# One hybrid streaming layer on one core: retention with one transposition and products in half-height pieces of the array, the keys' lower parts stored once, and the weight sums' results in PSUM banks of their own

## The chip, the core and the metric

The kernel runs on one core of a Trainium2 chip. The time is device time in microseconds (us), the median of several runs. Engines are named as in the profile: PE (TensorE: matmuls and transpositions), PEld (its weight loads), DVE (VectorE), ACT (ScalarE), POOL (GpSimd), SP (the queue that issues the DMAs).

## The reference

One layer over 1024 prompt frames and 32 sample frames, model width 1024, eight heads. What the change touches is the score product of the differential attention and the retention:

```python
qa = rmsnorm(qa.reshape(B, T, A_HEADS, 2, A_DIM), g_qn)      # A_DIM 64, two maps per head
ka = rmsnorm(ka.reshape(B, T, A_HEADS, 2, A_DIM), g_kn)
s = jnp.einsum('bqhcd,bkhcd->bhcqk', q_blk, ka) * scale      # chunk-causal mask, softmax, p0 - lam * p1
...
def retention_chunk(q, k, v, s0, d_mat, q_decay):            # R_DK 64, R_DV 128
    inner = jnp.einsum('...ihd,...jhd->...hij', q, k) * d_mat
    o = jnp.einsum('...hij,...jhe->...ihe', inner, v)
    return o + jnp.einsum('...ihd,...hde->...ihe', q, s0) * q_decay[:, :, None]
s_next = chunk_decay * s + einsum('jhd,jhe->hde', k * k_decay, v)
```

Around it stand a projection to 8192 columns ahead (one block of weights for attention and one for retention per head), and behind it the output projection, a SwiGLU of width 2816 and a gated embedding. Outputs are the layer's result, the keys and values, and the retention states.

## The kernel before

**Stages.** Up to about 1083 us runs one planned stage (`stream`): 72 attention units (head h, tile i; tiles 0 to 7 are 128 prompt frames each, tile 8 is the 32 sample frames) and 72 retention units four units behind. Behind it come the output projection and the SwiGLU's first half (`stream_bc`, to about 1660 us), then the rest.

**What sets the order.** Both stages are written as Python generators. A planner (`Flow`) runs at build time: each step yields an estimated cost on an engine (`V`, `S`, `G`, `M` for DVE, ACT, POOL, PE), or `get`/`put` of a buffer, and the order in which the planner starts the steps becomes the order of each engine's instructions. On the chip every engine runs its list in that order.

**Numbers in two parts.** Operands of the large products are split into an upper fp16 part and a lower one. A projected tile takes three fp16 matmuls per 128 rows of depth (L713 to L715).

**Attention unit** (`unit_a`, `attend`). The queries `q4[:, m]` of map m hold the upper part in one half of the partitions and the lower part in the other (map 0: upper in 0 to 63; map 1: upper in 64 to 127). The key tile `kT` has four planes: the upper part of each map, written into both halves, and the lower part of each map, again in both halves. Six fp16 transpositions (L1045) turn queries and keys. The scores of map m are one matmul over the upper plane (L850), on the diagonal a small matmul that adds the mask (L852), and one over the lower plane (L853), all 128 rows deep; keys are taken 512 at a time. Up to 512 keys (tiles 0 to 3) both maps go into the two banks of one `sc` tile, map 0 first; above that (tiles 4 to 8) each map has its own turn.

**Retention unit** (`retention`). All in fp32; a fp32 matmul shows as two records in the profile. `qk` holds queries and keys of a tile side by side (columns 0 to 127) and zeros behind them (128 to 191). Two transpositions (L1116, columns 0 to 127 and 64 to 191) and one copy of 256 columns (L1119) give `qT`: plane 0 one of them over the other, plane 1 the upper one's partner over zeros. The zeros make every product 128 rows deep: scores (L1126), queries times state (L1128, the state's lower 64 partitions are zeros too), and the state's increment (L1129, 128 columns of weights, of whose result half is used). L1134 adds scores times values.

**Scales in the second stage.** The sum of squares over the 128 partitions of a block of weights is one matmul of one column (`weight_scale`, L300). In `stream_bc` it writes column 511 of `ssb`, one PSUM bank for the whole stage, which also holds the RMSNorm's sums (L1543) and the scale row that L1558 writes and L1562 reads eight times.

Of the kernel before, what the change touches and what calls it, by code (L numbers as in the profile page):

```python
# [21 lines left out]
P = 128  # L22
# [48 lines left out]
def M(us):  # L71
    return {"M": us}
# [111 lines left out]
def kernel(  # L184
# [104 lines left out]
    def weight_scale(amax, n, gi, tag, pool=True, norm=False, total=False, at_bank=None):  # L289


        p2 = sm(n, tag + "p2", 3)
        if total:
            if at_bank is None:
                yield ("wait", "id")
            key, psum = at_bank or ("o", ps_o)
            yield ("get", key)
            yield M(0.06)
            ps = psum[:, 511:512] if at_bank else psum.tile([P, 512], F32, tag=key, name="mt")[:, 0:1]
            nc.tensor.matmul(out=ps, lhsT=ones16, rhs=amax, start=True, stop=True)  # L300
# [24 lines left out]
        return s, d  # L325
# [159 lines left out]
    with ExitStack() as pa:  # L485
# [38 lines left out]
        nc.gpsimd.memset(S2[64:128], 0.0)  # L524
        s02 = hp.tile([P, 2, P], F32, name="s02")
        nc.gpsimd.memset(s02[64:128], 0.0)

# [224 lines left out]
        def prep_head_a(h, w, e):  # L752
# [7 lines left out]
            s0 = s02[:, h % 2]  # L760
            nc.sync.dma_start(out=s0[0:64], in_=st0[h])
            gr = hp.tile([P, P], F32, tag="grn", name="grn", bufs=2)
# [9 lines left out]
        def cache_steps(h, dA, e):  # L772
# [46 lines left out]
            if h:  # L819
                yield ("wait", ("av", h - 1, NT - 1))  # L820
            kcs = hp.tile([P, 4, PAST], F16, tag="kcs", name="kcs")
# [17 lines left out]
        def attend(key, i, R, q4, sblocks, masked, vblocks, NK, sc_ap, do_ap):  # L839
# [3 lines left out]
            for ms in ((0, 1),) if NK <= 512 else ((0,), (1,)):  # L843
                yield ("get", "sc")
                yield M(len(ms) * (2 * NK / 2400.0 + 0.03))
                ps = ps_s.tile([P, 1024], F32, tag="sc", name="sc")
                for m in ms:
                    for b0, n, kts in sblocks:
                        o = ps[0:R, 512 * ms.index(m) + b0:512 * ms.index(m) + b0 + n]
                        nc.tensor.matmul(out=o, lhsT=q4[:, m, 0:R], rhs=kts[:, m], start=True, stop=False)  # L850
                        if masked and b0 + n == NK:
                            nc.tensor.matmul(out=o[:, n - 64:n], lhsT=mrow[:, 0:R], rhs=mneg, start=False, stop=False)  # L852
                        nc.tensor.matmul(out=o, lhsT=q4[:, m, 0:R], rhs=kts[:, 2 + m], start=False, stop=True)  # L853
                if m:
# [129 lines left out]
        def unit_a(h, i, ps, dA, e):  # L984
# [39 lines left out]
            if i == NT - 1:  # L1024
# [4 lines left out]
            yield S(384, 0.1)  # L1029
            st = wk.tile([P, 6, 2, 64], F16, tag="qst", name="qst")  # L1030
# [6 lines left out]
            nc.vector.tensor_tensor(out=st[0:R, 4:6], in0=zqk[:, 1].unsqueeze(2).broadcast_to([R, 2, 2, 64]),  # L1037
                                    in1=st[0:R, 2:4], op=ALU.subtract)
            yield ("put", "z")
            yield ("get", "o")  # L1040
            yield M(0.336)
            pt = ps_o.tile([P, 1024], F16, tag="o", name="t")
            ptv = pt[:, 0:768].rearrange("p (g c) -> p g c", g=6)
            for g in range(6):
                nc.tensor.transpose(out=ptv[:, g, 0:R], in_=st[0:R, g].rearrange("p a c -> p (a c)"), identity=id16[0:R, 0:R])  # L1045
# [63 lines left out]
        def retention(h, i, R, vr, e, box):  # L1109
            yield ("wait", ("rot", h, i))  # L1110
            yield ("get", "o")
            yield M(0.22)
            pr = ps_o.tile([P, 512], F32, tag="o", name="pr")

            for a in range(2):
                nc.tensor.transpose(out=pr[:, a * P:a * P + R], in_=qk[0:R, (h * NT + i) % NQ, 64 * a:64 * a + P], identity=id32[0:R, 0:R])  # L1116
# [7 lines left out]
            yield M(0.66)  # L1124
            por = ps_o.tile([P, 512], F32, tag="o", name="por")[0:R, 0:P]
            nc.tensor.matmul(out=pr[0:R, 256:256 + R], lhsT=qT[:, 0, 0:R], rhs=qT[:, 1, 0:R], start=True, stop=True)  # L1126
            if S_in is not None:
                nc.tensor.matmul(out=por, lhsT=qT[:, 1, 0:R], rhs=S_in, start=True, stop=False)  # L1128
            nc.tensor.matmul(out=pr[:, 384:512], lhsT=qk[0:R, (h * NT + i) % NQ, 0:P], rhs=vr[0:R], start=True, stop=True)  # L1129
            yield V(128)  # L1130
# [8 lines left out]
            Sn = S2[:, (h * NT + i) % 2]  # L1139
            Sq = Sn[0:64]  # L1140
            if S_in is None:
                nc.vector.tensor_scalar(out=Sq, in0=pr[0:64, 384:512], scalar1=gT, scalar2=None, op0=ALU.mult)
            else:
                nc.vector.tensor_tensor(out=Sq, in0=S_in[0:64], in1=pr[0:64, 384:512], op=ALU.add)
                yield V(128, 0.5)
                nc.vector.tensor_scalar(out=Sq, in0=Sq, scalar1=gT, scalar2=None, op0=ALU.mult)
# [286 lines left out]
    with ExitStack() as pc:  # L1433
# [18 lines left out]
        with ExitStack() as pw:  # L1452
# [8 lines left out]
            xfs, gus, dns, banks, done = [], {}, {}, {}, []  # L1461
            ssb = pss.tile([P, 512], F32, tag="ss", name="ss")

# [47 lines left out]
            def residual(c):  # L1511
# [28 lines left out]
                B = CW // 4  # L1540
                ps = ssb
                for b in range(4):
# [41 lines left out]
            def load_gu(j):  # L1584
# [47 lines left out]
            def load_dn(m):  # L1632
# [24 lines left out]
                nc.vector.tensor_tensor(out=am, in0=ams[:, 0:1], in1=ams[:, 1:2], op=ALU.add)  # L1657
                s, d = yield from weight_scale(am, 1, None, "dn", norm=True, total=True, at_bank=("sw", ssb))
                for st, js in sts:
# [159 lines left out]

            flow = Flow(dict(ps=7, ss=1, sw=1, w=3, st=2, pr=2, th=2, acc=2, sq=2))  # L1820
            del flow.buffers["w"][1:], flow.buffers["st"][1:]
# [209 lines left out]
```

## Time and profile before

| | |
|---|---|
| median of 3 runs | 1945.02 us (1944.85 to 1945.72) |
| profiled execution: time, and span from the first to the last instruction | 1944.48 us, 1942.7 us |
| busy: PE, DVE, ACT, POOL | 97%, 78%, 55%, 35% |
| matmul records | 14267 |
| DMA: traffic over the span | 147.43 MB, 76 GB/s |

The busy time of PE counts a matmul from its start to its modelled end, and these overlap: a matmul of 512 fp16 columns shows 0.38 us, but the next one starts 0.22 us behind it. So what a matmul costs on PE is read here from the distance between starts in the timeline, not from its duration. Forms are written K*M KxN: K rows and M columns of weights, K rows by N columns of moving data.

### The profile page before, as it was taken

How to read it: one execution, taken by the hardware profiler on the slowest of the kernel's cores; microseconds unless marked ns; L12 is line 12 of the kernel's file. 1: busy time of each engine (PE TensorE's matmuls, PEld its weight loads, DVE VectorE, ACT ScalarE, POOL GpSimd, SP SyncE). 2: the span in 40 equal slices, each digit the busy share in tenths (PEclk: the TensorE clock that was granted, in tenths of full speed). 3: DMA queues.
4: the chain of work that ended last, by engine and by line, in shares of the span. 5: the costliest groups of instructions: out<-in, count | busy, mean ns of one | idle time of the engine just before them, and what ended most of it. 6: DMA issues, size and time to landing. Idle time of an engine off the chain costs nothing.

```text
span 1942.7 us, 38400 instructions
## 1 busy us (share of the span) xinstructions
PE 1886.0 (97%) x14267; PEld 1219.2 (63%) x14267; DVE 1511.3 (78%) x3947; ACT 1065.4 (55%) x2788; POOL 688.8 (35%) x1169
## 2 busy tenths in 40 slices
PE   6899999999999999999999998999999999999999
PEld 3465555655555555556566685777777776666665
DVE  7888878787787777877887579999999986753364
ACT  6766666666666666665666345555555552111132
POOL 2654435454444454444542058322323210000010
PEclk9999999999999999999999998999999999999999
DMA  6222112111121121221113721222111107211031
GB/s 205 70 64 75 62 28 63 57 49 63 33 79 57 31 82 36 55 80 29 61 57 132 267 68 34 78 89 86 69 66 45 66 31 266 73 61 64 24 131 49
DMA packets 71947, 147.43 MB, mean 76 GB/s; under 512 B 25264, under 2 KB 52016, under 8 KB 63824
## 3 DMA queue, kind: packets, MB, share of 16 engines
q1 hardware_dynamic: 71760, 144.98, 22.4%
q8 instruction: 112, 1.84, 0.4%
q14 instruction: 75, 0.61, 0.1%
HBM read 113.61 MB, written 31.34 MB: 75 GB/s over the span
## 4 chain that ended last, share of the span: by engine, by line
PE 77%; DVE 11%; POOL 5%; ACT 4%; issue 2%; DMA 1%; SPq 0%; POOLq 0%; DVEq 0%; ACTq 0%
PE ps L471 9%; PE ps L472 9%; PE ps L473 9%; PE pj L713 8%; PE pj L715 8%; PE pj L714 8%; PE ps L1448 4%; PE ps L1447 4%; PE ps L1446 4%; ACT p L868 2%; PE sc L850 1%; PE t L897 1%; PE sc L853 1%; POOL qkr L749 1%; DVE nm L860 1%
## 5 line engine op out<-in xcount | busy, mean ns | idle before, releaser
L713 PE MATMUL pj<-w,xh 128*128 128x512 f16 x1024 | 390.1, 381 | 0.0
L714 PE MATMUL pj<-w,xh 128*128 128x512 f16 x1024 | 389.5, 380 | 0.0
L715 PE MATMUL pj<-w,xh 128*128 128x512 f16 x1024 | 389.3, 380 | 0.0
L471 PE MATMUL ps<-mixs,w 128*128 128x352 f16 (+1 forms) x960 | 261.9, 278 | 1.2 <-ACT pws L1324 1.2
L472 PE MATMUL ps<-mixs,w 128*128 128x352 f16 (+1 forms) x960 | 261.9, 278 | 0.0
L473 PE MATMUL ps<-mixs,w 128*128 128x352 f16 (+1 forms) x960 | 261.8, 278 | 0.0
L471 PEld LDWEIGHTS <-w 128*128 128x128 f16 x1728 | 170.2, 98 | 63.9 <-ACT mixs L1478 6.4
L473 PEld LDWEIGHTS <-w 128*128 128x128 f16 x1728 | 170.0, 98 | 54.2 <-issue 2.7
L472 PEld LDWEIGHTS <-w 128*128 128x128 f16 x1728 | 169.9, 98 | 51.7 <-issue 2.2
L715 PEld LDWEIGHTS <-xh 128*128 128x128 f16 x1024 | 100.4, 98 | 121.9 <-issue 1.7
L1581 POOL TENSOR_TENSOR st<-st 128x512 f32<-128x512 f32 x66 | 85.8, 1301 | 251.1 <-DVE w L1576 187.0
L868 ACT ACTIVATE p<-sc,nb,scs 128x256 f32<-128x256 f32 (+7 forms) x128 | 106.1, 829 | 83.3 <-POOL nb L862 61.1
L713 PEld LDWEIGHTS <-xh 128*128 128x128 f16 x1024 | 101.2, 99 | 76.3 <-issue 2.8
L472 PE MATMUL ps<-tT,w 128*128 128x352 f16 (+1 forms) x528 | 143.7, 277 | 2.6 <-DVE tT L1472 2.6
L714 PEld LDWEIGHTS <-xh 128*128 128x128 f16 x1024 | 100.4, 98 | 71.7 <-issue 1.1
L471 PE MATMUL ps<-tT,w 128*128 128x352 f16 (+1 forms) x528 | 143.8, 277 | 0.0
L473 PE MATMUL ps<-tT,w 128*128 128x352 f16 (+1 forms) x528 | 143.6, 277 | 0.0
L1576 DVE SCALAR_TENSOR_TENSOR w<-st,gus,w 128x512 f16<-128x512 f32 x132 | 140.5, 1065 | 0.1
L860 DVE TENSOR_REDUCE nm<-sc 128x2 f32<-128x256 f32 (+6 forms) x112 | 102.7, 917 | 24.1 <-PE sc L853 22.0
L1448 PE MATMUL ps<-a,w 128*128 128x352 f16 x312 | 97.5, 313 | 0.5 <-DVE w L1667 0.5
L1446 PE MATMUL ps<-a,w 128*128 128x352 f16 x312 | 97.5, 312 | 0.0
L1447 PE MATMUL ps<-a,w 128*128 128x352 f16 x312 | 97.5, 312 | 0.0
(430 smaller groups left out, 4856.1 us busy)
## 6 DMA issues: line engine op xcount, KB each, us to landing
st<-in_win_dram SPq DMA_DIRECT2D x30, 1024.0 KB, 5.0
st<-in_wgu_dram SPq DMA_DIRECT2D x22, 1024.0 KB, 4.9
st<-in_wdn_dram SPq DMA_DIRECT2D x16, 704.0 KB, 4.6
out_dram<-kv SPq DMA_DIRECT2D x64, 128.0 KB, 1.7
a_d<-a SPq DMA_DIRECT2D x9, 528.0 KB, 2.7
b<-a_d SPq DMA_DIRECT2D x9, 528.0 KB, 8.9
mixs<-mix_d SPq DMA_DIRECT2D x8, 528.0 KB, 5.8
pw_d<-pws SPq DMA_DIRECT2D x12, 352.0 KB, 5.0
```

Of the source, the lines that this page charges most:

```text
L471: nc.tensor.matmul(out=ps, lhsT=wh, rhs=ah, start=first, stop=False)
L472: nc.tensor.matmul(out=ps, lhsT=wh, rhs=al, start=False, stop=False)
L473: nc.tensor.matmul(out=ps, lhsT=wl, rhs=ah, start=False, stop=last)
L713: nc.tensor.matmul(out=ps, lhsT=xhi, rhs=w[:, k, 0], start=(k == 0), stop=False)
L714: nc.tensor.matmul(out=ps, lhsT=xhi, rhs=w[:, k, 1], start=False, stop=False)
L715: nc.tensor.matmul(out=ps, lhsT=xh[:, k, 1, t0:t0 + P], rhs=w[:, k, 0], start=False, stop=(k == KD - 1))
L860: nc.vector.tensor_reduce(out=nm[0:R, mc], in_=pv, axis=AX.X, op=ALU.max, negate=True)
L868: nc.scalar.activation(pt[0:R, 0:NK], ps[0:R, p0:p0 + NK], AF.Exp, bias=nb[0:R, m:m + 1], scale=sc_ap[0:R], accum_out=Z[0:R, m:m + 1])
L1446: nc.tensor.matmul(out=ps, lhsT=wt[:, 0, j], rhs=a[:, 0, cs], start=(first and j == js[0]), stop=False)
L1447: nc.tensor.matmul(out=ps, lhsT=wt[:, 1, j], rhs=a[:, 0, cs], start=False, stop=False)
L1448: nc.tensor.matmul(out=ps, lhsT=wt[:, 2, j], rhs=a[:, 1, cs], start=False, stop=(last and j == js[-1]))
L1576: nc.vector.scalar_tensor_tensor(out=w[:, i, 1], in0=src, scalar=s, in1=w[:, i, 0], op0=ALU.mult, op1=ALU.subtract)
```

## The change

1. **Keys' lower parts once.** `kT` and `kcs` have three planes: the third holds map 0's lower part in partitions 0 to 63 and map 1's in 64 to 127. Five transpositions, not six; the subtraction for the lower keys is 128 columns, not 256; the copy into `kT` 384, not 512. The lower product (L853) of map m is 64 rows deep, in rows 0 to 63 or 64 to 127, and with up to 512 keys both maps' lower products stand next to each other, behind both upper ones and masks.
2. **Retention.** One transposition; two copies (64 and 128 partitions of 128 columns, the first from partitions 64 to 127 to 0 to 63). Scores are 64 rows deep in rows 0 to 63, queries times state 64 rows deep in rows 64 to 127. The increment has 64 columns of weights and writes partitions 64 to 127, where the state now lies. The zero columns and three memsets on POOL go.
3. **Scales.** L300 of the second stage writes a PSUM tile of its own: one of the seven `ps` banks for the gate/up blocks 0 to 3, a new tile of the `ss` bank for the later ones.

```diff
-            ps = psum[:, 511:512] if at_bank else psum.tile([P, 512], F32, tag=key, name="mt")[:, 0:1]
+            ps = psum.tile([P, 512], F32, tag=key, name="mt")[:, 0:1]
...
-        kT = hp.tile([P, 4, T], F16, name="kT")
+        kT = hp.tile([P, 3, T], F16, name="kT")
...
-        qk = hp.tile([P, NQ, 192], F32, name="qk")
-        nc.gpsimd.memset(qk[:, :, P:], 0.0)
+        qk = hp.tile([P, NQ, P], F32, name="qk")
...
-                nc.vector.scalar_tensor_tensor(out=kcs[:, 2 + m], in0=kc[:, m], scalar=s[:, 0:1], in1=kcs[:, m],
+                mp = slice(64 * m, 64 * m + 64)
+                nc.vector.scalar_tensor_tensor(out=kcs[mp, 2], in0=kc[mp, m], scalar=s[mp, 0:1], in1=kcs[mp, m],
...
-                for m in ms:
-                    for b0, n, kts in sblocks:
-                        o = ps[0:R, 512 * ms.index(m) + b0:512 * ms.index(m) + b0 + n]
+                for b0, n, kts in sblocks:
+                    os = [ps[0:R, 512 * j + b0:512 * j + b0 + n] for j in range(len(ms))]
+                    for m, o in zip(ms, os):
                         nc.tensor.matmul(out=o, lhsT=q4[:, m, 0:R], rhs=kts[:, m], start=True, stop=False)
                         if masked and b0 + n == NK:
                             nc.tensor.matmul(out=o[:, n - 64:n], lhsT=mrow[:, 0:R], rhs=mneg, start=False, stop=False)
-                        nc.tensor.matmul(out=o, lhsT=q4[:, m, 0:R], rhs=kts[:, 2 + m], start=False, stop=True)
+                    for m, o in zip(ms, os):
+                        mp = slice(64 * m, 64 * m + 64)
+                        nc.tensor.matmul(out=o, lhsT=q4[mp, m, 0:R], rhs=kts[mp, 2], start=False, stop=True)
...
-            yield V(384, 1.0, 0.07)
+            yield V(256, 1.0, 0.07)
...
-            nc.vector.tensor_tensor(out=st[0:R, 4:6], in0=zqk[:, 1].unsqueeze(2).broadcast_to([R, 2, 2, 64]),
-                                    in1=st[0:R, 2:4], op=ALU.subtract)
+            nc.vector.tensor_tensor(out=st[0:R, 4], in0=zqk[:, 1], in1=st[0:R, 2:4, 0], op=ALU.subtract)
...
-            for g in range(6):
+            for g in range(5):
                 nc.tensor.transpose(out=ptv[:, g, 0:R], in_=st[0:R, g].rearrange("p a c -> p (a c)"), identity=id16[0:R, 0:R])
...
-            g = yield either(V(512, 0.5), S(512, -0.09))
-            copy(g, kT[:, :, t0:t0 + R], ptv[:, 2:6, 0:R])
+            g = yield either(V(384, 0.5), S(384, -0.09))
+            copy(g, kT[:, :, t0:t0 + R], ptv[:, 2:5, 0:R])
...
-            for a in range(2):
-                nc.tensor.transpose(out=pr[:, a * P:a * P + R], in_=qk[0:R, (h * NT + i) % NQ, 64 * a:64 * a + P], identity=id32[0:R, 0:R])
+            nc.tensor.transpose(out=pr[:, 0:R], in_=qk[0:R, (h * NT + i) % NQ], identity=id32[0:R, 0:R])
             qT = wk.tile([P, 2, P], F32, tag="qT", name="qT")
-            g = yield either(V(256), S(256, -0.06))
-            copy(g, qT[:, :, 0:R], pr[:, 0:2 * P].rearrange("p (a c) -> p a c", a=2)[:, :, 0:R])
+            g = yield either(V(128), S(128, -0.06))
+            copy(g, qT[0:64, 1, 0:R], pr[64:128, 0:R])
+            g = yield either(V(128), S(128, -0.06))
+            copy(g, qT[:, 0, 0:R], pr[:, 0:R])
...
-            nc.tensor.matmul(out=pr[0:R, 256:256 + R], lhsT=qT[:, 0, 0:R], rhs=qT[:, 1, 0:R], start=True, stop=True)
+            nc.tensor.matmul(out=pr[0:R, 256:256 + R], lhsT=qT[0:64, 0, 0:R], rhs=qT[0:64, 1, 0:R], start=True, stop=True)
             if S_in is not None:
-                nc.tensor.matmul(out=por, lhsT=qT[:, 1, 0:R], rhs=S_in, start=True, stop=False)
-            nc.tensor.matmul(out=pr[:, 384:512], lhsT=qk[0:R, (h * NT + i) % NQ, 0:P], rhs=vr[0:R], start=True, stop=True)
+                nc.tensor.matmul(out=por, lhsT=qT[64:128, 0, 0:R], rhs=S_in[64:128], start=True, stop=False)
+            nc.tensor.matmul(out=pr[64:128, 384:512], lhsT=qk[0:R, (h * NT + i) % NQ, 0:64], rhs=vr[0:R], start=True, stop=True)
...
-                ps = ssb
+                ps = pss.tile([P, 512], F32, tag="ss", name="ss")
...
-                s, d = yield from weight_scale(am, 1, 1, "gu", norm=True, total=True, at_bank=("sw", ssb))
+                s, d = yield from weight_scale(am, 1, 1, "gu", norm=True, total=True, at_bank=("ps", psb) if j < 4 else ("ss", pss))
```

How the instructions move. The first place is on PE, the scores of a unit with 384 keys (tile 2). A row has the line, the operation, the result <- its operands, and rows by columns of the result. Before:

```order
L850 MATMUL sc<-kT,q_816 128x384
L852 LDWEIGHTS mrow
L852 MATMUL sc<-mneg,mrow 128x64
L853 LDWEIGHTS q_816
L853 MATMUL sc<-kT,q_816 128x384
L850 LDWEIGHTS q_816
L850 MATMUL sc<-kT,q_816 128x384
L852 LDWEIGHTS mrow
L852 MATMUL sc<-mneg,mrow 128x64
L853 LDWEIGHTS q_816
L853 MATMUL sc<-kT,q_816 128x384
```

The same place of the changed kernel, where L848 is the upper product, L850 the mask and L853 the lower product:

```order
L848 MATMUL sc<-kT,q_811 128x384
L850 LDWEIGHTS mrow
L850 MATMUL sc<-mneg,mrow 128x64
L848 LDWEIGHTS q_811
L848 MATMUL sc<-kT,q_811 128x384
L850 LDWEIGHTS mrow
L850 MATMUL sc<-mneg,mrow 128x64
L853 LDWEIGHTS q_811
L853 MATMUL sc<-kT,q_811 128x384
L853 LDWEIGHTS q_811
L853 MATMUL sc<-kT,q_811 128x384
```

The lower products moved together behind the upper ones. In units with more than 512 keys the order stays (upper, lower, upper, mask, lower, map by map), and only the depth of the lower products is another.

The second place is on PE, the products of a full retention unit from the middle of the stage, with their neighbours. Before:

```order
L715 MATMUL pj<-w,xh 128x512
L1126 MATMUL pr<-qT 128x128
L1128 MATMUL por<-S_131,qT 128x128
L1129 MATMUL pr<-vr,qk 128x128
L916 LDWEIGHTS aT
```

And of the changed kernel:

```order
L853 MATMUL sc<-kT,q_9769 128x512
L1126 MATMUL pr<-qT 128x128
L1128 MATMUL por<-S_130,qT 128x128
L1129 MATMUL pr<-vr,qk 64x128
L916 LDWEIGHTS aT
```

The three products still follow one another; what stands ahead of them differs from unit to unit, since the planner's costs changed.

The third place is on PE, at the end of the output projection, where the second L300 of the second stage stands. Before:

```order
L473 MATMUL ps<-mixs,w 128x176
L300 LDWEIGHTS cst_sb
L300 MATMUL ss<-wamh,cst_sb 128x1
L471 LDWEIGHTS w
L471 MATMUL ps<-mixs,w 128x352
```

And of the changed kernel:

```order
L473 MATMUL ps<-mixs,w 128x176
L300 LDWEIGHTS cst_sb
L300 MATMUL mt<-wamh,cst_sb 128x1
L471 LDWEIGHTS w
L471 MATMUL ps<-mixs,w 128x352
```

It stands at the same place of PE's list and writes another bank (`mt`, not `ss`). In the whole second stage PE's list is otherwise the same as before.

More of the change, by code (lines that the diff above doesn't have):

```diff
@@ L760, in prep_head_a @@
             s0 = s02[:, h % 2]
-            nc.sync.dma_start(out=s0[0:64], in_=st0[h])
+            nc.sync.dma_start(out=s0[64:128], in_=st0[h])
             gr = hp.tile([P, P], F32, tag="grn", name="grn", bufs=2)
@@ L820, in cache_steps @@
                 yield ("wait", ("av", h - 1, NT - 1))
-            kcs = hp.tile([P, 4, PAST], F16, tag="kcs", name="kcs")
+            kcs = hp.tile([P, 3, PAST], F16, tag="kcs", name="kcs")
             vcs = hp.tile([P, 4, 2, P], F16, tag="vcs", name="vcs")
@@ L1029, in unit_a @@
             yield S(384, 0.1)
-            st = wk.tile([P, 6, 2, 64], F16, tag="qst", name="qst")
+            st = wk.tile([P, 5, 2, 64], F16, tag="qst", name="qst")
             zqk = z[0:R].rearrange("p a (m c) -> p a m c", m=2)
@@ L1034, in unit_a @@
             nc.scalar.copy(st[0:R, 2:4], zqk[:, 1].unsqueeze(2).broadcast_to([R, 2, 2, 64]))
-            yield V(384, 1.0, 0.07)
+            yield V(256, 1.0, 0.07)
             nc.vector.tensor_tensor(out=sf[:, 1:3], in0=zqk[:, 0], in1=sf[:, 0:4:3], op=ALU.subtract)
-            nc.vector.tensor_tensor(out=st[0:R, 4:6], in0=zqk[:, 1].unsqueeze(2).broadcast_to([R, 2, 2, 64]),
-                                    in1=st[0:R, 2:4], op=ALU.subtract)
+            nc.vector.tensor_tensor(out=st[0:R, 4], in0=zqk[:, 1], in1=st[0:R, 2:4, 0], op=ALU.subtract)
             yield ("put", "z")
             yield ("get", "o")
-            yield M(0.336)
+            yield M(0.28)
             pt = ps_o.tile([P, 1024], F16, tag="o", name="t")
-            ptv = pt[:, 0:768].rearrange("p (g c) -> p g c", g=6)
-            for g in range(6):
+            ptv = pt[:, 0:640].rearrange("p (g c) -> p g c", g=5)
+            for g in range(5):
                 nc.tensor.transpose(out=ptv[:, g, 0:R], in_=st[0:R, g].rearrange("p a c -> p (a c)"), identity=id16[0:R, 0:R])
@@ L1111, in retention @@
             yield ("get", "o")
-            yield M(0.22)
+            yield M(0.11)
             pr = ps_o.tile([P, 512], F32, tag="o", name="pr")
-            for a in range(2):
-                nc.tensor.transpose(out=pr[:, a * P:a * P + R], in_=qk[0:R, (h * NT + i) % NQ, 64 * a:64 * a + P], identity=id32[0:R, 0:R])
+            nc.tensor.transpose(out=pr[:, 0:R], in_=qk[0:R, (h * NT + i) % NQ], identity=id32[0:R, 0:R])
             qT = wk.tile([P, 2, P], F32, tag="qT", name="qT")
-            g = yield either(V(256), S(256, -0.06))
-            copy(g, qT[:, :, 0:R], pr[:, 0:2 * P].rearrange("p (a c) -> p a c", a=2)[:, :, 0:R])
+            g = yield either(V(128), S(128, -0.06))
+            copy(g, qT[0:64, 1, 0:R], pr[64:128, 0:R])
+            g = yield either(V(128), S(128, -0.06))
+            copy(g, qT[:, 0, 0:R], pr[:, 0:R])
             if h or i:
@@ L1123, in retention @@
             yield ("get", "o")
-            yield M(0.66)
+            yield M(0.5)
             por = ps_o.tile([P, 512], F32, tag="o", name="por")[0:R, 0:P]
-            nc.tensor.matmul(out=pr[0:R, 256:256 + R], lhsT=qT[:, 0, 0:R], rhs=qT[:, 1, 0:R], start=True, stop=True)
+            nc.tensor.matmul(out=pr[0:R, 256:256 + R], lhsT=qT[0:64, 0, 0:R], rhs=qT[0:64, 1, 0:R], start=True, stop=True)
             if S_in is not None:
-                nc.tensor.matmul(out=por, lhsT=qT[:, 1, 0:R], rhs=S_in, start=True, stop=False)
-            nc.tensor.matmul(out=pr[:, 384:512], lhsT=qk[0:R, (h * NT + i) % NQ, 0:P], rhs=vr[0:R], start=True, stop=True)
+                nc.tensor.matmul(out=por, lhsT=qT[64:128, 0, 0:R], rhs=S_in[64:128], start=True, stop=False)
+            nc.tensor.matmul(out=pr[64:128, 384:512], lhsT=qk[0:R, (h * NT + i) % NQ, 0:64], rhs=vr[0:R], start=True, stop=True)
             yield V(128)
@@ L1139, in retention @@
             Sn = S2[:, (h * NT + i) % 2]
-            Sq = Sn[0:64]
+            Sq = Sn[64:128]
             if S_in is None:
-                nc.vector.tensor_scalar(out=Sq, in0=pr[0:64, 384:512], scalar1=gT, scalar2=None, op0=ALU.mult)
+                nc.vector.tensor_scalar(out=Sq, in0=pr[64:128, 384:512], scalar1=gT, scalar2=None, op0=ALU.mult)
             else:
-                nc.vector.tensor_tensor(out=Sq, in0=S_in[0:64], in1=pr[0:64, 384:512], op=ALU.add)
+                nc.vector.tensor_tensor(out=Sq, in0=S_in[64:128], in1=pr[64:128, 384:512], op=ALU.add)
                 yield V(128, 0.5)
@@ L1461 @@
             xfs, gus, dns, banks, done = [], {}, {}, {}, []
-            ssb = pss.tile([P, 512], F32, tag="ss", name="ss")
             def span(c):
@@ L1657, in load_dn @@
                 nc.vector.tensor_tensor(out=am, in0=ams[:, 0:1], in1=ams[:, 1:2], op=ALU.add)
-                s, d = yield from weight_scale(am, 1, None, "dn", norm=True, total=True, at_bank=("sw", ssb))
+                s, d = yield from weight_scale(am, 1, None, "dn", norm=True, total=True, at_bank=("ss", pss))
                 for st, js in sts:
@@ L1818, in stream_bc @@
                             down_mm(halves[m, c], dns[m][0], js, c, js[0] < 16, False)
-            flow = Flow(dict(ps=7, ss=1, sw=1, w=3, st=2, pr=2, th=2, acc=2, sq=2))
+            flow = Flow(dict(ps=7, ss=1, w=3, st=2, pr=2, th=2, acc=2, sq=2))
             del flow.buffers["w"][1:], flow.buffers["st"][1:]
```

2 lines of the change are left out of this document (removed).

## The prediction

> **What bounds the kernel now.** I read the page's totals first, then the stages, then the timeline of PE.
>
> ```profile
> span 1942.7 us, 38400 instructions
> PE 1886.0 (97%) x14267; PEld 1219.2 (63%) x14267; DVE 1511.3 (78%) x3947; ACT 1065.4 (55%) x2788; POOL 688.8 (35%) x1169
> PE 77%; DVE 11%; POOL 5%; ACT 4%; issue 2%; DMA 1%; SPq 0%; POOLq 0%; DVEq 0%; ACTq 0%
> ```
>
> PE is busy 97% of the span and has 77% of the chain that ended last. By stages (window, its length, then busy us of PE, PEld, DVE, ACT, POOL, and the granted clock):
>
> ```profile
> 80.00:1083.00 1003.00, 991.64 (x7259) 580.46 (x7258) 795.88 (x2421) 656.26 (x1939) 458.98 (x921) 1.00 0.20 62
> 1165.00:1195.00 30.00, 21.16 (x174) 15.07 (x172) 27.95 (x58) 16.92 (x41) 23.36 (x23) 0.88 0.06 19
> 1195.00:1265.00 70.00, 64.27 (x536) 48.63 (x535) 68.56 (x147) 40.13 (x91) 34.45 (x38) 0.95 0.21 72
> ```
>
> In the first stage, once it is filled, PE idles 1003.00 - 991.64 = 11.4 us in 1003. So almost every nanosecond that PE's list gains or loses there is one of the kernel's. From 1165 to 1265 us DVE is the fuller engine (27.95 of 30, 68.56 of 70) and PE waits.
>
> How long PE needs for an instruction is the distance between starts. Three rows of a retention unit, and what follows them:
>
> ```profile
> 608.43 0.39 PE L1126 MATMUL pr<-qT 128*128 128x128 f32 x2
> 608.65 0.39 PE L1128 MATMUL por<-S,qT 128*128 128x128 f32 x2
> 608.88 0.39 PE L1129 MATMUL pr<-vr,qk 128*128 128x128 f32 x2
> 609.10 0.38 PE L713 MATMUL pj<-w,xh 128*128 128x512 f16 x1
> ```
>
> Each fp32 product is two passes, 0.22 us in all, and nothing stands between them: 0.67 us for the three.
>
> **The price that decides.** The change makes products 64 rows deep or 64 columns wide. Before has a few small ones among full ones:
>
> ```profile
> 1118.39 0.31 PE L473 MATMUL ps<-mixs,w 128*128 128x352 f16 x1
> 1118.54 0.71 PE L1543 MATMUL ss<-cst_sb,acc 128*88 128x1 f32 x8
> ...
> 1185.52 0.31 PE L473 MATMUL ps<-mixs,w 128*128 128x352 f16 x1
> 1185.76 0.49 PE L1543 MATMUL ss<-cst_sb,acc 128*44 128x1 f32 x8
> ...
> 1189.48 0.31 PE L472 MATMUL ps<-tT,w 128*128 128x352 f16 x1
> 1189.63 0.31 PE L473 MATMUL ps<-tT,w 128*128 128x352 f16 x1
> 1189.87 0.56 PE L1558 MATMUL ss<-dg,cst_sb 44*128 44x176 f32 x2
> 1190.37 0.32 PE L471 MATMUL ps<-tT,w 128*128 128x352 f16 x1
> ```
>
> A full product of 352 columns is followed by the next after 0.15 us (1189.48 to 1189.63), and so it is by one with 88 columns of weights (1118.39 to 1118.54). By one with 44 columns it is followed after 0.24 us, by one 44 rows deep after 0.24 us too. The built program gives every matmul a piece of the array, 32, 64 or 128 rows by 32, 64 or 128 columns; 88 takes the full piece, 44 one of 64. So **a change of piece costs 0.24 - 0.15 = 0.09 us** on PE. A second part comes to it, the load of the first weights, which nothing covers after such a change:
>
> ```profile
> 142.55 0.18 PE L853 MATMUL sc<-kT,q 128*32 128x32 f16 x1
> 142.65 0.49 PE L1126 MATMUL pr<-qT 128*128 128x128 f32 x2
> 142.98 0.39 PE L1128 MATMUL por<-S,qT 128*128 128x128 f32 x2
> ```
>
> Here L1126 comes behind a 32-column piece and takes 0.33 us, not 0.22: 0.11 us of open weight load for fp32 weights of 128 columns. For fp16 it is about 0.01 us (behind L1558, L471's duration is 0.32, not 0.31). The way back costs the same: from 1189.87 to 1190.37, open load 0.11, two passes of 176 fp32 columns at 0.15 (128 take 0.11), and 0.09 for the change make the 0.50 us that stand there. The Trainium skill, "TensorEngine Tiling (Array Packing)", section "Tiling Modes", says that changing the tiling mode drains the engine, while a move to another tile of the same mode does not; the trace agrees, at 0.09 us for each change.
>
> **Part by part.** I counted neighbours of different pieces in the built program's matmuls, without fp32 transpositions to few columns, which show no pause: 234 before, 735 after. Of the 501 more, 340 lie at the lower products: two in a unit with up to 512 keys (in, out), eight in one with more (in and out for two blocks of two maps), 40 per head, and some 2 or 3 in the sample unit. 158 lie in the retention: into 64x128, on to 128x64 for the increment, back to full, three in each of 64 full units but where a neighbour already has that piece; the sample units had as many before.
>
> - Changes of piece: 501 x 0.09 us = **+45.1 us**.
> - Open weight loads: retention about 64 x (0.11 for the scores + 0.05 for the increment, half the columns) less what was there before, +7.4 us; at the lower products 340 x 0.01 and some fp32 neighbours, +6.5; others +1.0. **+14.9 us**.
> - Transpositions:
>
> ```profile
> L1116 PE MATMUL pr<-cst_sb,qk 128*128 128x128 f32 x128 | 24.8, 276 | 0.0
> L1045 PE MATMUL t<-id,qst 128*128 128x128 f16 x384 | 33.4, 221 | 0.6 <-DVE qst L1037 0.4
> ...
> 601.40 0.50 PE L1045 MATMUL t<-id,qst 128*128 128x128 f16 x6
> 601.74 0.38 PE L713 MATMUL pj<-w,xh 128*128 128x512 f16 x1
> 606.13 0.38 PE L1116 MATMUL pr<-cst_sb,qk 128*128 128x128 f32 x2
> 606.35 0.38 PE L713 MATMUL pj<-w,xh 128*128 128x512 f16 x1
> ```
>
> Six fp16 ones take 0.34 us, two fp32 ones 0.22. Away go 64 x 0.11 + 64 x 0.056 and 16 small ones: **-11.0 us**. Depth or width alone saves no time: a pass's time is that of its moving columns, and those stay.
>
> - Two products beside each other. With up to 512 keys the two lower products lie in different rows and banks; if the second runs wholly beside the first, it saves 0.05, 0.11, 0.16 and 0.21 us for tiles 0 to 3 (0.056 per 128 columns, as the fp16 rows above), 0.53 us per head, 4.3 us; else nothing. I take 4.3: fp16 weight loads are short (0.01 us open), so nothing keeps the second back. Scores and state product of the retention: between 0 and 64 x 0.22 = 14 us. Their order is both passes of the one, then both of the other, and in the row of 142.65 a weight load takes as long as a pass (0.11), so four loads one after another would leave nothing to gain. One pass beside another would be 7 us; I take half of that, **-7.8 us** with the pair above. No row of before shows such a pair.
> - Waits of PE in the first stage that the later PE takes up:
>
> ```profile
> PE t L1208 <- DVE mx L1203: 3.6, 9, 0.7
> PE pj L740 <- DVE su L737: 1.8, 4, 0.5
> ```
>
> They are short waits for chains on DVE; a unit that PE finishes 0.7 us later leaves these chains that time. At most the 11.4 us go, and new ones may come, for the planner still counts the three products at less than before; I take **-5 us**.
> - DVE and ACT: two copies into `qT` in place of one, against a subtraction and a copy of 128 columns less.
>
> ```profile
> L388 ACT COPY qT<-pr 128x256 f32<-128x256 f32 x46 | 17.1, 372 | 20.5 <-PE pr L1116 20.1
> L388 ACT COPY qT<-pr 128x64 f32<-128x64 f32 x8 | 1.7, 214 | 0.5 <-PE pr L1116 0.2
> ```
>
> By these rows one of 128 columns is about 267 ns, so two are 0.16 us more than one, 72 times, on engines at 796 and 656 of 1003 us. PE does other units' work meanwhile: 0. Without that cover it would be 72 x 0.16 = 12 us. The memsets at the start go from POOL, which waits there for ACT: 0.
> - The scales' bank:
>
> ```profile
> PE ss L300 <- DVE xf L1562: 8.4, 2, 6.3
> PE ss L300 <- DVE wamh L1605: 3.2, 3, 2.1
> ...
> 1161.01 0.39 DVE L1524 SCALAR_TENSOR_TENSOR xf<-ps,o0d,xf 128x176 f32<-128x176 f32 x1
> 1176.18 0.14 DVE L1605 TENSOR_TENSOR wamh<-gam 128x1 bf16<-128x1 f32 x1
> 1179.19 0.38 DVE L1562 SCALAR_TENSOR_TENSOR xf<-xf,gS,ss 128x176 f32<-128x176 f32 x1
> ```
>
> The 8.4 us are L300 waiting until L1562 has read the shared bank, and they go. Next late at the longer one is L1605, L300's own operand, at 1176.18 (the last L1562 read ends near 1179.57), and then what DVE, full for 27.95 of 30 us, has in its unchanged list. PE gets what DVE gains where it waits for PE now, its 2 idle us of those 30: **-2 us**, between 0 and -8.4. The bank that L300 takes there from the seven is the one that L1524 read at 1161.01, seven allocations back, so the new wait costs 0; without that lead it would be up to the next L1524.
>
> Sum: 45.1 + 14.9 - 11.0 - 7.8 - 5 - 2 = **+34.2 us**. The profiled execution took 1944.48 us (1.8 around the span of 1942.7), which makes 1978.7; the median shown lies 0.5 higher. I say 1979.
>
> **The rivals.** *Nothing overlaps and no wait is taken up*: 45.1 + 14.9 - 11.0 = +49.0, 1994 us. For it: weight loads as long as passes, few waits to take up; against it: the pairs' separate rows and banks.
>
> *All overlaps, all waits taken up*: 49.0 - 18.3 - 11.4 - 8.4 = +10.9, 1956 us. Against it: DVE's fullness at 1165 to 1265.
>
> *Faster, because these switches cost less than those in the trace*: L1558 is fp32 and alone; between fp16 products of a unit the change of piece could hide under the next weight load. With all overlaps and the scales' wait, savings are 11.0 + 18.3 + 8.4 = 37.7 us; over 501 changes, the kernel is faster if one costs less than 0.075 us with its open load, and at no cost it takes 1907 us. Against it: 0.09 us stands at each row above, with fp16 behind and ahead, in rows and in columns. The Trainium skill, "TensorE: Matmul & The Clock Gate", Part 3, has products in different rows run together, four of a quarter's depth at 3.07 times the speed; no run so far shows it. By it alone both kinds of pair would overlap in full, 10.5 us more than I take, 1969 us.
>
> *The change does not do what it says*: if products of half depth ran like full ones, only -11.0 and -2 would be left, 1932 us; the 44-row row speaks against it.
>
> **How the numbers follow.** The forecast (1966 to 1988) 0.62, no overlap (to 1999) 0.17, all overlaps (from 1956) 0.10, faster for either reason 0.08, no change (within 0.2%, what a measurement of this kernel can tell) 0.03. The range 1956 to 1999 leaves out the faster cases and a little above.
>
> **What would show it.** Starts of L853 0.09 us later than the columns ahead give, and as much behind it, four times each in a unit with over 512 keys; L1126 to the product behind L1129 at about 1.0 us, not 0.67; the first stage some 36 us longer; L300's wait for L1562 gone. Starts of the second lower product some ns behind the first would show the overlap. Wrong it would be if L853 followed without the 0.09 us, or if PE then waited for the two copies.

## The result, and the profile after

The changed kernel took 1964.65 us, median of 4 runs (1964.25 to 1965.38), beside 1945.28 us of the kernel before in the same comparison (4 runs). The ratio is 1.01, with a 95% interval from 1.0082 to 1.0117: slower, by 19.4 us at the medians. The forecast was 1979 in a range of 1956 to 1999.

The totals of the page of the changed kernel, and its chain of work that ended last:

```profile
span 1962.5 us, 38142 instructions
PE 1909.2 (97%) x14123; PEld 1184.4 (60%) x14123; DVE 1534.1 (78%) x3997; ACT 1076.2 (55%) x2836; POOL 663.1 (34%) x1140
PE 84%; DVE 9%; POOL 2%; ACT 2%; issue 1%; DMA 1%; SPq 0%; DVEq 0%; POOLq 0%; ACTq 0%
```

PE has 144 matmuls fewer and is busy 1909.2 - 1886.0 = 23.2 us longer; its share of the chain went from 77% to 84%. The span grew by 19.8 us. The stages, as windows (window, its length, busy us of PE, PEld, DVE, ACT, POOL, and the granted clock); the first stage now ends where the first L471 of the second starts, at 1104.0 (before at 1082.7), and the two later windows are moved by the same 22 us:

```profile
80.00:1104.00 1024.00, 1016.09 (x7107) 546.86 (x7104) 820.14 (x2469) 667.47 (x1989) 435.37 (x897) 1.00 0.19 62
1187.00:1217.00 30.00, 23.25 (x188) 16.29 (x186) 29.10 (x59) 18.15 (x44) 24.88 (x25) 0.94 0.06 19
1217.00:1287.00 70.00, 61.58 (x542) 47.90 (x541) 69.18 (x151) 39.74 (x91) 33.02 (x35) 0.98 0.24 83
```

The loss lies in the first stage, which is 21.3 us longer; what stands behind it is 1.5 us shorter. PE is not busy there for 7.9 us of 1024, where it was 11.4 of 1003: no engine keeps it waiting more, its own list takes longer. DVE (820.14) and ACT (667.47) have room, and no wait of PE in this stage is for the two copies into `qT`. From 1187 to 1287 us DVE is still the fuller engine.

The timeline of PE (start, duration, engine, line) at a retention unit whose neighbours are full products. Each fp32 product of 64 rows stands as two records:

```profile
519.04 0.49 PE L897 MATMUL t<-cst_sb,p 128*128 128x128 f32 x3
519.46 0.37 PE L1126 MATMUL pr<-qT 64*128 64x128 f32 x1
519.47 0.37 PE L1128 MATMUL por<-S,qT 64*128 64x128 f32 x1
519.67 0.27 PE L1126 MATMUL pr<-qT 64*128 64x128 f32 x1
519.68 0.27 PE L1128 MATMUL por<-S,qT 64*128 64x128 f32 x1
519.88 0.43 PE L1129 MATMUL pr<-vr,qk 128*64 128x128 f32 x2
520.25 0.39 PE L848 MATMUL sc<-kT,q 128*128 128x512 f16 x1
```

Scores (L1126, rows 0 to 63) and state product (L1128, rows 64 to 127) start 0.01 us apart, pass by pass: the second is free. From the first to the product behind the increment it is 0.79 us where it was 0.67, and the change ahead of it costs 0.095 more.

The lower products of a unit with 384 keys, and of one with 640 (two blocks, 512 and 128):

```profile
320.05 0.19 PE L850 MATMUL sc<-mneg,mrow 128*128 128x64 bf16 x1
320.17 0.34 PE L853 MATMUL sc<-kT,q 64*128 64x384 f16 x2
320.44 0.33 PE L721 MATMUL pj<-xs,w 128*128 128x64 f16 x6
...
605.76 0.38 PE L712 MATMUL pj<-w,xh 128*128 128x512 f16 x1
605.97 0.38 PE L848 MATMUL sc<-kT,q 128*128 128x512 f16 x1
606.28 0.39 PE L853 MATMUL sc<-kT,q 64*128 64x512 f16 x1
606.60 0.23 PE L848 MATMUL sc<-kT,q 128*128 128x128 f16 x1
606.67 0.19 PE L850 MATMUL sc<-mneg,mrow 128*128 128x64 bf16 x1
606.80 0.23 PE L853 MATMUL sc<-kT,q 64*128 64x128 f16 x1
606.95 0.39 PE L710 MATMUL pj<-w,xh 128*128 128x512 f16 x1
```

At 320.17 the two lower products (x2) last 0.34 us together, 0.01 more than one alone, and PE goes on after 0.27: 0.16 for one product's columns and 0.10 for the change of piece. At 605.97 a full product of 512 columns, followed after 0.21 where another full one stands behind it (605.76 to 605.97), is followed after 0.31 by L853, and that after 0.32 by the next: some 0.10 us at each of the four borders, and nothing beside it.

The waits of PE behind 1104 us (what waited, for whom, us in total, times, longest):

```profile
PE mt L300 <- DVE wamh L1604: 7.1, 4, 3.1
PE ps L472 <- DVE tT L1471: 2.9, 1, 2.9
PE ps L472 <- POOL mixs L1471: 2.4, 1, 2.4
PE ss L1542 <- DVE gus L315: 1.7, 1, 1.7
```

L300's 8.4 us for L1562 are gone, and nearly all of them have come back under other names: its own operand `wamh`, then POOL and DVE. These four waits make 14.1 us; before, L300's two (8.4 and 3.2) and L472's for `tT` (2.6) made 14.2.

### The profile page after: what moved, and what is told of

Its sections match the earlier page's. It is cut to its first block, busy times and chain, and to the rows that moved or that the text cites. A ratio compares the mean times of both kernels' runs of the same rounds, so it can differ in the third digit from the quotient of the medians.

```text
span 1962.5 us, 38142 instructions
## 1 busy us (share of the span) xinstructions
PE 1909.2 (97%) x14123; PEld 1184.4 (60%) x14123; DVE 1534.1 (78%) x3997; ACT 1076.2 (55%) x2836; POOL 663.1 (34%) x1140
## 4 chain that ended last, share of the span: by engine, by line
PE 84%; DVE 9%; POOL 2%; ACT 2%; issue 1%; DMA 1%; SPq 0%; DVEq 0%; POOLq 0%; ACTq 0%
PE pj L710 10%; PE pj L712 9%; PE pj L711 9%; PE ps L471 9%; PE ps L472 9%; PE ps L473 9%; PE ps L1448 4%; PE ps L1446 4%; PE ps L1447 4%; PE sc L853 2%; PE sc L848 2%; PE t L897 2%; PE pj L721 1%; PE pr L1129 1%; PE po L916 1%
## 5 line engine op out<-in xcount | busy, mean ns | idle before, releaser
L472 PE MATMUL ps<-mixs,w 128*128 128x352 f16 (+1 forms) x960 | 260.9, 277 | 2.4 <-POOL mixs L1471 2.4
L471 PE MATMUL ps<-mixs,w 128*128 128x352 f16 (+1 forms) x960 | 261.0, 277 | 1.5 <-DVE pws L1326 1.5
L471 PEld LDWEIGHTS <-w 128*128 128x128 f16 x1728 | 169.8, 98 | 60.8 <-issue 5.5
L472 PEld LDWEIGHTS <-w 128*128 128x128 f16 x1728 | 169.6, 98 | 49.7 <-issue 0.8
L710 PEld LDWEIGHTS <-xh 128*128 128x128 f16 x1024 | 100.9, 99 | 91.8 <-issue 13.5
L472 PE MATMUL ps<-tT,w 128*128 128x352 f16 (+1 forms) x528 | 143.6, 277 | 2.9 <-DVE tT L1471 2.9
L471 PE MATMUL ps<-tT,w 128*128 128x352 f16 (+1 forms) x528 | 143.6, 277 | 0.0
L860 DVE TENSOR_REDUCE nm<-sc 128x1 f32<-128x768 f32 (+6 forms) x112 | 103.1, 921 | 47.3 <-PE sc L853 45.8
L862 POOL TENSOR_SCALAR nb<-nm,scs 128x1 f32<-128x1 f32 (+1 forms) x76 | 30.0, 395 | 241.4 <-DVE nm L860 236.6
L1448 PE MATMUL ps<-a,w 128*128 128x352 f16 x312 | 97.5, 313 | 0.5 <-DVE w L1666 0.5
L1446 PE MATMUL ps<-a,w 128*128 128x352 f16 x312 | 97.5, 312 | 0.0
```

The lines of the kernel that those rows point to most:

```text
L471: nc.tensor.matmul(out=ps, lhsT=wh, rhs=ah, start=first, stop=False)
L472: nc.tensor.matmul(out=ps, lhsT=wh, rhs=al, start=False, stop=False)
L710: nc.tensor.matmul(out=ps, lhsT=xhi, rhs=w[:, k, 0], start=(k == 0), stop=False)
L860: nc.vector.tensor_reduce(out=nm[0:R, mc], in_=pv, axis=AX.X, op=ALU.max, negate=True)
L1446: nc.tensor.matmul(out=ps, lhsT=wt[:, 0, j], rhs=a[:, 0, cs], start=(first and j == js[0]), stop=False)
L1448: nc.tensor.matmul(out=ps, lhsT=wt[:, 2, j], rhs=a[:, 1, cs], start=False, stop=(last and j == js[-1]))
```

## The experiments

Each was timed beside the kernel before on its chip (1944.3 to 1945.3 us in the batches); ratios are to that.

**Each part alone.** The keys' part (planes, transpositions, lower products), with retention and scales as before:

```diff
-                        nc.tensor.matmul(out=o, lhsT=q4[:, m, 0:R], rhs=kts[:, 2 + m], start=False, stop=True)
+                    for m, o in zip(ms, os):
+                        mp = slice(64 * m, 64 * m + 64)
+                        nc.tensor.matmul(out=o, lhsT=q4[mp, m, 0:R], rhs=kts[mp, 2], start=False, stop=True)
```

> Before with the keys' part of the change alone (three key planes, lower products 64 rows deep, five transpositions). Theory (each change of the array's piece costs 0.09 to 0.10 us of PE, pairs overlap in full): 367 more changes, +34.5 us of PE work less what waits take up, so 1968 to 1976 us, and most of the change's loss lies here. Rival (the loss comes from retention's two copies and its longer chain): no more than 1946 us, since DVE has less to do here.

With 64 rows the lower product takes the lower keys with the upper queries alone; the product of the two lower parts, which the kernel before adds, falls away, in the changed kernel and in the versions with zeros too.

Measured: 1972.99 us, ratio 1.0143 (1.0126 to 1.016), some 28.5 us slower, as the theory had it.

The retention's part alone:

```diff
-            nc.tensor.matmul(out=pr[0:R, 256:256 + R], lhsT=qT[:, 0, 0:R], rhs=qT[:, 1, 0:R], start=True, stop=True)
+            nc.tensor.matmul(out=pr[0:R, 256:256 + R], lhsT=qT[0:64, 0, 0:R], rhs=qT[0:64, 1, 0:R], start=True, stop=True)
             if S_in is not None:
-                nc.tensor.matmul(out=por, lhsT=qT[:, 1, 0:R], rhs=S_in, start=True, stop=False)
+                nc.tensor.matmul(out=por, lhsT=qT[64:128, 0, 0:R], rhs=S_in[64:128], start=True, stop=False)
```

> Before with the retention part of the change alone. Theory: 185 more changes of piece and open fp32 weight loads against one transposition less and a full overlap of scores and state product, +8 us of PE work, so 1947 to 1953 us. Rival (copies and chain): 1960 us or more, with PE waiting for qT's copies or DVE.

Measured: 1950.05 us, ratio 1.0026 (1.0015 to 1.0037), some 5.5 us slower, in the range expected.

The scales' part alone:

```diff
-            ps = psum[:, 511:512] if at_bank else psum.tile([P, 512], F32, tag=key, name="mt")[:, 0:1]
+            ps = psum.tile([P, 512], F32, tag=key, name="mt")[:, 0:1]
```

> Before with the scales' banks of the change alone. Theory (DVE is full at that place): the 8.4 us of L300's wait for L1562 go, and waits for DVE and POOL take most of their place, as in the changed kernel: 1942 to 1944 us. Rival (the wait was lost time): 1936 to 1938 us.

Measured: 1943.5 us, ratio 0.9995 (0.9986 to 1.0004). The interval includes no gain at all. The rival, that the whole wait would be gained, falls: the waits of PE in the second stage have the names that they have in the changed kernel,

```profile
PE mt L300 <- DVE wamh L1604: 5.1, 2, 3.1
PE ps L472 <- DVE tT L1471: 3.6, 1, 3.6
PE ps L472 <- POOL mixs L1471: 1.8, 1, 1.8
```

in place of the 8.4 us for L1562. With the 1.7 us for `gus`, which this trace has too, they make 12.2 us, 2.0 less than before. DVE is nearly full there (27.95 of 30 us before), and PE waits for it at one place or another.

The three apart make 28.5 + 5.5 - 1.1 = 32.9 us, and together they cost 19.4. The parts help one another; the records show how. Neighbouring matmul records of different pieces are 292 before, 357 more with the keys' part, 184 more with the retention's, and 498 more with both, not 541. In 25 of the 64 full retention units the first product stands directly behind a lower product, which in the changed kernel has the same piece. The 43 changes fewer are some 4 us of the 13.5; the rest is about what fp32 weight loads that stand open behind a change cost in the two parts alone and no longer cost together (the numbers stand under the table below). Such a place in the changed kernel:

```profile
358.14 0.19 PE L850 MATMUL sc<-mneg,mrow 128*128 128x64 bf16 x1
358.26 0.28 PE L853 MATMUL sc<-kT,q 64*128 64x256 f16 x1
358.27 0.37 PE L1128 MATMUL por<-S,qT 64*128 64x128 f32 x1
358.38 0.27 PE L1126 MATMUL pr<-qT 64*128 64x128 f32 x1
358.48 0.27 PE L1128 MATMUL por<-S,qT 64*128 64x128 f32 x1
358.49 0.27 PE L1126 MATMUL pr<-qT 64*128 64x128 f32 x1
358.69 0.43 PE L1129 MATMUL pr<-vr,qk 128*64 128x128 f32 x2
359.06 0.23 PE L916 MATMUL po<-vh,aT 128*128 128x128 f16 x1
```

L853 here has rows 0 to 63. L1128, in rows 64 to 127, starts 0.01 us behind it, with no change of piece between and its weights loaded, and the scores follow when L853's columns are through. So it is in 13 of the 25 places; in most of the others, where the lower product has 128 columns, the scores are first and start some 0.01 us behind its columns. In PE's list L1126 stands ahead of L1128 everywhere. The section on the kernel before has every engine run its list in that order; for products in different rows the starts in these 13 places do not keep it.

**The overlap taken away.** The changed kernel with the state in partitions 0 to 63, so that scores, state product and the increment's result have the same rows; the order of PE's list stays:

```diff
-                nc.tensor.matmul(out=por, lhsT=qT[64:128, 0, 0:R], rhs=S_in[64:128], start=True, stop=False)
-            nc.tensor.matmul(out=pr[64:128, 384:512], lhsT=qk[0:R, (h * NT + i) % NQ, 0:64], rhs=vr[0:R], start=True, stop=True)
+                nc.tensor.matmul(out=por, lhsT=qT[0:64, 1, 0:R], rhs=S_in[0:64], start=True, stop=False)
+            nc.tensor.matmul(out=pr[0:64, 384:512], lhsT=qk[0:R, (h * NT + i) % NQ, 0:64], rhs=vr[0:R], start=True, stop=True)
```

> The changed kernel with the state in partitions 0 to 63, so that queries times state read the same rows of the array as the scores and cannot run beside them; PE's list of instructions is the same, one for one. Theory (the two overlap in full, 0.22 us a unit, 63 units): 12 to 14 us over the changed kernel, 1977 to 1979 us. Rival (weight loads one after another leave no overlap): within 3 us of the changed kernel.

Measured: 1978.29 us, ratio 1.0172 (1.0156 to 1.0187), 13.6 us over the changed kernel: the overlap in full. L1126 starts ahead of L1128 in every full unit here, and the increment takes 0.36 us as it did, though its result moved to partitions 0 to 63. The same unit as the one at 519.46 above:

```profile
526.07 0.49 PE L897 MATMUL t<-cst_sb,p 128*128 128x128 f32 x3
526.49 0.48 PE L1126 MATMUL pr<-qT 64*128 64x128 f32 x2
526.81 0.38 PE L1128 MATMUL por<-S,qT 64*128 64x128 f32 x2
527.13 0.43 PE L1129 MATMUL pr<-vr,qk 128*64 128x128 f32 x2
527.49 0.39 PE L848 MATMUL sc<-kT,q 128*128 128x512 f16 x1
```

Here the three take 1.00 us, the "about 1.0" of the prediction; with the rows apart they took 0.79. The difference, 0.21, is one whole product.

**The savings without the changes of piece.** One transposition less in each, as the change has it, but planes filled up with zeros, so that every product keeps 128 rows; the scales' part too. The third plane's halves go to two planes, and `qT` gets its zeros once:

```diff
+        qT2 = hp.tile([P, 2, 2, P], F32, name="qT2")
+        nc.gpsimd.memset(qT2[64:128, :, 1], 0.0)
...
-            for a in range(2):
-                nc.tensor.transpose(out=pr[:, a * P:a * P + R], in_=qk[0:R, (h * NT + i) % NQ, 64 * a:64 * a + P], identity=id32[0:R, 0:R])
+            nc.tensor.transpose(out=pr[:, 0:R], in_=qk[0:R, (h * NT + i) % NQ], identity=id32[0:R, 0:R])
...
+            for m in range(2):
+                mp = slice(64 * m, 64 * m + 64)
+                copy(g, kT[mp, 2 + m, t0:t0 + R], ptv[mp, 4, 0:R])
```

> The change with every product kept 128 rows deep: one transposition less for the keys and one for retention, lower key planes and the second qT plane filled up with zeros that are written once, scales' banks as in the change. No more changes of piece than before, no overlap. Theory: -10.7 us of PE work and -2 at the scales, so 1931 to 1937 us, faster than both kernels. Rival (extra copies and chain cost the time): these copies are all still there and two more for the keys, so 1950 us or more.

Measured: 1945.78 us, ratio 1.0005 (0.9996 to 1.0015). This missed: nothing was gained. Its first stage, and its longest wait of PE there:

```profile
80.00:1082.00 1002.00, 983.86 (x7128) 570.40 (x7126) 815.81 (x2538) 672.31 (x2034) 451.88 (x912) 1.00 0.20 63
...
PE t L1215 <- POOL mx L1210: 7.4, 6, 1.4
```

PE's busy time fell by 991.64 - 983.86 = 7.8 us, and its idle time rose from 11.4 to 18.1. L1215 is the last transposition of a mixed tile; in the planned order it now stands too early for what POOL gives it, six times, and holds up all behind it.

Only retention's transposition of these, with the scales' part and the keys as before:

> Before with retention's one transposition and two copies, all products 128 rows deep (the second qT plane filled up with zeros), and the scales' banks; the keys as before. PE work falls by 6.8 us. Theory now, after e3: PE's saved work comes back as waits for DVE and POOL, so 1938 to 1944 us with PE idle in the first stage above before's. Rival (the keys' two further copies alone ate e3's gain): 1936 us or less, with PE idle as before.

Measured: 1942.21 us, ratio 0.999 (0.9981 to 0.9999), in the range expected; PE idles 13.4 us of the 1001 from 80 to 1081, above the 11.4 of before, as expected too.

Now the lower products of the version with zeros made 64 rows deep, in units with more than 512 keys alone. No transposition, copy or order is changed:

```diff
-                        nc.tensor.matmul(out=o, lhsT=q4[:, m, 0:R], rhs=kts[:, 2 + m], start=False, stop=True)
+                        mp = slice(64 * m, 64 * m + 64) if NK > 512 else slice(0, P)
+                        nc.tensor.matmul(out=o, lhsT=q4[mp, m, 0:R], rhs=kts[mp, 2 + m], start=False, stop=True)
```

> e3 with one edit: in units with more than 512 keys (and the sample unit) the lower products read 64 rows, not 128. Nothing else differs: same copies, same order, no pair beside another. Theory: 301 changes of piece at 0.09 to 0.10 us and open loads of 0.01, so 25 to 32 us over e3, less some waits. Rival (the price is not paid in this place, it hides under the next weight load): the time of e3 within 3 us.

Measured: 1969.67 us, ratio 1.0126 (1.0111 to 1.0141), 23.9 us over the version with zeros. The records have 592 neighbours of different pieces against 288. By these two traces the 304 more cost 31.3 us, neighbours of the same piece some 4 more, and the waits gave 11 back. A few rows of it:

```profile
607.98 0.38 PE L853 MATMUL sc<-kT,q 128*128 128x512 f16 x1
608.29 0.39 PE L857 MATMUL sc<-kT,q 64*128 64x512 f16 x1
608.61 0.23 PE L853 MATMUL sc<-kT,q 128*128 128x128 f16 x1
```

L857 is the lower product here: the same 0.31 and 0.32 us as in the changed kernel. The depth alone makes the loss, and it saves nothing.

**The wait that ate the savings.** The version with zeros, with one number of the planner changed, the delay it allows ahead of that last transposition:

```diff
-            yield ("delay", 0.4)
+            yield ("delay", 1.5)
```

> e3 with one number of the planner changed: the last transposition of a unit (L1215 there) is planned 1.5 us behind its operand, not 0.4. Same instructions. Theory (e3's gain went into PE waiting at that transposition for POOL, 7.4 us): these waits go, 1936 to 1941 us. Rival (DVE's load sets the pace, not that place): the waits move to other places, 1944 us or more.

Measured: 1930.58 us, ratio 0.993 (0.9916 to 0.9943): faster than both kernels, and some 5 us below the expected range. Its first stage is over at 1070.6 us, 12.1 us earlier than before:

```profile
80.00:1071.00 991.00, 983.15 (x7133) 569.05 (x7132) 811.09 (x2545) 678.12 (x2053) 455.21 (x900) 1.00 0.20 63
```

PE's busy time is as low as without the delay (983), and its idle time is 7.9 us in place of 18.1. Whether that is the delay's work alone, two more kernels say, the same number in the kernel before and in the changed one:

> The kernel before with one number changed, the planner's delay ahead of the last transposition of a mixed tile (0.4 to 1.5). PE's work stays as it is. Theory (the full pieces save 11 us of PE work, the delay only takes PE's waits for the mixed tile away): at most the 6.2 us that PE waits there before can go, 1938 to 1944 us. Rival (the delay alone explains what the version with full pieces and the longer delay gained): 1929 to 1934 us.

Measured: 1945.43 us, ratio 1.0004 (0.9995 to 1.0013), just above what was expected; the rival is far off. The wait for the mixed tile went, and others took its place:

```profile
PE t L1045 <- DVE qst L1036: 2.5, 5, 0.6
PE t L1045 <- DVE aT L908: 1.7, 1, 1.7
PE po L920 <- DVE aT L908: 1.3, 3, 0.4
```

> The changed kernel with the same number changed (0.4 to 1.5). Theory (the loss of the change is PE work at changes of piece, and its PE waits only 1.5 us for the mixed tile in the first stage): 1961 to 1967 us. Rival (the change loses by its order, which the longer delay mends): below 1955 us.

Measured: 1967.54 us, ratio 1.0121 (1.0105 to 1.0136), half a us above the expected range. The longer delay does not mend the changed kernel's loss. There is little waiting to mend: its PE idles 7.9 us of the 1024 from 80 to 1104, and 6.4 with the delay.

So the transpositions saved are worth having, and in these versions become time only together with the delay; neither shows a gain alone. The longer delay gives the planner another order of the whole stage, and which of the shifts in it counts was not followed further than the wait of L1215.

## Why the prediction was right, and where its sizes were off

The sign, the engine and the mechanism were right: the first stage has PE full, and what the change adds there is changes of piece. The forecast of +34.2 us was 14.4 too much by the profiled spans, and the time lies just below the 1966 to 1988 that had a chance of 0.62, in the stretch that was given 0.10 as "all overlaps". That rival has the overlaps nearly right (18.3 us, against 17.0 in the table), but it takes up 19.8 us of waits, against 4.7, and keeps 14.9 us of open loads, against 3.6; its two errors offset each other in part, so that the time fell into its stretch is partly luck and bears out its overlaps alone.

Summed over all neighbouring matmul records of the two traces (each distance between starts, less 0.417 ns per moving column, as the projections' 512 columns have it, and twice that in a record of fp32; distances with an idle gap over 0.1 us count as waits), the terms stand so:

| term | predicted | in the records |
|---|---|---|
| changes of piece | +45.1 (501) | +48.7 (498) |
| open weight loads | +14.9 | +3.6 |
| transpositions (columns) | -11.0 | -10.8 |
| two products beside each other | -7.8 | -17.0 |
| waits, both stages | -5 - 2 | -4.7 |
| sum | +34.2 | +19.8 (the spans' difference) |

- **Changes of piece**: 0.09 us was worked out from a few rows and came as 0.095 to 0.105 (medians of like neighbours, into and out of a piece of 64). That cheap switches would make it faster is out: the version that differs in them alone lost 23.9 us.
- **Transpositions**: as predicted.
- **Two products beside each other** is one of the two steps that failed: "One pass beside another would be 7 us; I take half of that". The reason given, that four loads one after another would leave nothing to gain, did not hold. The rows of 519.46 show both passes of both products in the time of one, their weight loads included, and taking the rows away cost 13.6 us. The pairs of lower products came in full, as taken (4.2 us): the second starts 3 to 4 ns behind the first, 32 times. The Trainium skill's page "TensorE: Matmul & The Clock Gate", Part 3, which the prediction weighed, has products in different rows run together; the trace agrees, with 0.01 us between the starts.
- **Open weight loads**, "+14.9 us", is the other, and the larger miss (11.3 us against 9.2). For a unit among full products the size was about right (1.00 us for the three, as predicted, when nothing overlaps). But 25 of 64 units stand directly behind a lower product, where the prediction's text allowed for a change less ("but where a neighbour already has that piece") and not for a load less. The version with the same rows, where nothing overlaps, shows that load: from the start of L1126 to the increment it is 0.53 to 0.59 us in 19 such places, and 0.64 elsewhere. Apart, the two parts show 4.3 and 8.9 us in this term, together 3.6. And the 7.5 us put down for lower products and other neighbours did not come, beyond the 0.008 us by which a change is dearer than 0.09.
- **Waits**: the two terms, -7 us, came as -4.7. In the first stage PE idles 3.5 us less (11.4 to 7.9), not 5. At the scales' bank L300's wait went and its operand was next late, as said; what stands behind the first stage is 1.5 us shorter, where 2 was taken.
- **The copies**: 0, as predicted. The changed kernel's first stage has no wait of PE for `qT`.
- Of what was to be seen: the borders of L853 are at +0.10 us, four times; the first stage is 21 us longer, not 36; the three products with what stands ahead take 0.88 us, not 1.09.

## What to carry to other kernels

On a full TensorE, count how often neighbouring matmuls change the shape of their piece before halving a product's depth or width: the halves save no columns, and each change costs as much as 230 fp16 columns. By these prices small pieces would pay only when they are gathered, pairs in different rows next to each other and same shapes in a row; no version here gains by it, so that is not shown. And work taken off the bounding engine is time only if the order lets it: look at the waits that come up in its place before judging the saving.

## What the runs showed of the hardware

- Two fp32 products in different halves of the rows run pass beside pass, 0.01 us apart, weight loads included; the second is free (0.79 us against 1.00).
- A product behind one of the same shape in the other rows can start 0.01 us after it, even fp32 behind fp16 (358.26 and 358.27), and ahead of a product that stands before it in PE's list (L1128 at 358.27, L1126 at 358.38; in 13 places).
- A change of shape to or from a piece of 64 costs 0.095 to 0.105 us either way, whether the depth or the width changes, and whether fp16 or fp32 stands behind it.
